# Reading back attention weights in whole rows, reordered first products and a shorter Newton chain in a hybrid decoder step

## The chip, the core and the metric

The kernel runs on one core of a Trainium2 chip. The core has TensorE (PE in the profile; its weight loads are PEld), VectorE (DVE), ScalarE (ACT), GpSimd (POOL) and SyncE (SP), which here issues nearly all transfers, and 16 DMA engines that move the data. The metric is the device time of one execution in microseconds; lower is better.

## What is computed

One layer of a decoder in float32, for a prompt of 512 tokens and for 8 running sequences ("samples") with one new token each. One projection of x (1024 columns) by `w_in` gives the inputs of two mixers; a second one by `w_out` and a layer norm end the layer:

```python
h = jnp.einsum('btd,de->bte', x, w_in)
qa, ka, va, za, ga, qb, kb, vb, gb = jnp.split(h, split_points, axis=-1)
log_a = log_sigmoid(za @ w_alpha2 + b_alpha) / GATE_TEMP
o_a, s_new = gla_chunked(qa, ka, va, log_a, s0, chunk)        # mixer A: gated linear attention, 4 heads
o_a = o_a * lax.rsqrt(jnp.mean(jnp.square(o_a), axis=-1, keepdims=True) + RMS_EPS) * gla_norm_g
o_b = dilated_attention(qb, k_all, v_all, q_idx, rel_bias)    # mixer B: 8 heads, three dilated windows
mix = jnp.concatenate([o_a * silu(ga), o_b * silu(gb)], axis=-1)
x_new = layer_norm(DEEPNORM_ALPHA * x + mix @ w_out, ln_g, ln_b)
```

In mixer B a sample's one query meets 256 cached keys per head (those that the three windows reach, gathered on the host in a fixed order) and its own new key. Its output is the sum of 256 cached value rows, weighted by the softmax.

## The kernel before

**Products in three parts.** Each float32 operand is split on the chip into a high part (`hi`, `xh`; ScalarE rounds to float32r) and a rest (`lo`, `xl`; VectorE subtracts), by `split` at line 412. A product is then three matmuls (`three`, line 608): high by high, high by rest, rest by high.

**The stages.** `dense` (line 681) is TensorE's main program: `ka` first, then the forget gate's `za`, then `qa`, `qb`, `kb`, `vb`, `gb`, `va`, `ga` and the output projection. For `ka` the loop goes over eight row blocks k of the contraction, and in each over two halves u of the tokens and two halves i of the columns, as their loads arrive (`first_loads` and `first_splits`, lines 536 and 563, with the list `FIRST`). All other weights come through two raw buffers (`weight_loads`, line 506): a load, the split, the next load. Beside this run the prompt's GLA (`gla_*`), its dilated attention (`strips`, `scores`, `softmax`, `weighted`, lines 1096 to 1208), and the samples' work.

**What sets the order.** Every piece of work is a generator that yields its instructions. `Plan.run` (line 300) keeps a model of the engines with a fixed cost for each instruction and each transfer (`Op`, line 77) and always issues the instruction that could begin first by that model, then the one of the lowest priority number. So the order on each engine is fixed when the program is built; on the chip an engine takes its instructions in that order, and one that waits holds those behind it. SyncE too has one order, and its transfers go into one queue on each DMA engine. All instructions are issued at line 359, so in the profile groups are told apart by the names of their tiles. Buffers come from pools of slots (`SLOTS`, line 58): a load waits until the slot's last user is done.

**The samples' attention.** `sample_queries` and `sample_logit` (lines 1211 and 1222) multiply cached keys with the queries on GpSimd and sum them on VectorE into `lt`. `sample_softmax` (line 1231) puts the logits together on TensorE (`ps_sl`), exponentiates and scales them: `p_s` has 64 partitions, row b*8 + h for sample b and head h, with 256 cached keys and one new one. Line 1269 stores it to the DRAM tile `psd_s`. `sample_values` (line 1284) then, for each sample `bi`, loads the cached values `vv` (128 partitions: h2*64 + d for head 2m + h2 and feature d; 4 x 256 elements for m and key) and the weights `pb` in the same layout, each row of weights repeated over 64 partitions: two loads, one for each h2. `sample_value` (line 1297) multiplies `vv` by `pb` on GpSimd in four pieces of 256, and VectorE sums over the keys into `o_pv`. `vv` and `pb` take two of the four `sv` slots, so two samples are in work at a time. After the eighth `o_pv`, `o_bs` and `mix_sample_b` follow; the output projection needs them, and also the samples' GLA (`sample_gla`, line 1307), whose buffers `s4` and `v4` use the same four slots.

A DRAM side of a transfer is written as a list of [step, count], outermost first. The attention bias strips, which `strips` loads to 128 partitions, have the side `[[T_P - 16, 8], [T_P - 1, 16], [1, w]]` (line 1107): 8 by 16 rows of w elements. The old `pb` loads have `[[0, 64], [512, 4], [1, 256]]`.

**The norms.** `rsqrt` (line 388) computes a reciprocal root as exp(-0.5 ln x) on ScalarE with one Newton step. For the layer norm of the prompt (`norm`, line 1560) the step is on ScalarE, while VectorE centres the rows (`between`); elsewhere it is on VectorE.

Of the kernel before, what the change touches and what calls it, by code (L numbers as in the profile page):

```python
# [11 lines left out]
F32 = mybir.dt.float32  # L12
# [10 lines left out]
KT = DM // P  # L23
# [29 lines left out]
T_D = 512  # L53
T_W = T_D + 258

N_WARM = 8

SLOTS = dict(
# [305 lines left out]
def trunk(ctx: ExitStack, tc: tile.TileContext, xT, xp, xs, state, ck, cv, w_in, wab, gnorm,  # L364
# [23 lines left out]
    def rsqrt(o, x, scale, eps, between=None):  # L388

        t = yield Need("m", "newton", [P, size(x)])  # L390
        t = t[:x.ap[0][1]]
        yield V.tensor_scalar(x, x, scale, eps, op0=ALU.mult, op1=ALU.add)
        yield S.activation(o, x, AF.Ln)
        yield S.activation(o, o, AF.Exp, scale=-0.5)
        if between:

            add(between, 5)
            yield S.activation(t, o, AF.Square)
            yield S.mul(t, t, x)
            yield S.activation(t, t, AF.Copy, scale=-0.5, bias=1.5)  # L400
            yield S.mul(o, o, t)
        else:
            yield V.tensor_tensor(t, o, o, op=ALU.mult)
            yield V.tensor_tensor(t, t, x, op=ALU.mult)
            yield V.tensor_scalar(x, o, -0.5, None, op0=ALU.mult)
            yield V.scalar_tensor_tensor(o, t, -3.0, x, op0=ALU.add, op1=ALU.mult)
        free(t)
# [31 lines left out]
    tabr = dram.tile([HB, T_R, T_P], F32, name="tabr")  # L439
    vad = dram.tile([NB, 512], F32, name="vad")  # L440
    qsd = dram.tile([NB, 512], F32, name="qsd")
    psd_s = dram.tile([64, 256], F32, name="psd_s")
    B = {}

    def make(key, need, n=1):
# [58 lines left out]
    order = [g for k, g in groups.items() if k not in ("ka0", "ka1")] + wo  # L504

    def weight_loads():
        for g in order:
            for i in range(g.parts):
                yield from g.load(i)

# [25 lines left out]
    def first_loads():  # L536
        za = w_in[:, OFF["za"]:OFF["za"] + 16].rearrange("(k p) n -> p k n", p=P)
        for n, a, *b in FIRST:
            if n == "x":
                c = b[0] if b else slice(0, NT)  # L540
                if a % 2 == 0 and c.start == 0:
                    xraw.append((yield Need("g", f"x_raw{a}", [P, 2, NT])))
                yield D.dma_start(xraw[a // 2][:, a % 2, c], xT[a * P:(a + 1) * P, c])
            else:
                if a % 4 == 0:
                    ka_raw.append((yield Need("r", f"raw_ka{a}", [P, 4, GW])))
                rows = w_in[a * P:b[0] * P, OFF["ka"]:OFF["ka"] + GW]
                yield D.dma_start(ka_raw[a // 4][:, a % 4:a % 4 + b[0] - a, :], rows.rearrange("(k p) n -> p k n", p=P))
            mark("first")
        yield D.dma_start(zw[:, :, :16], za)  # L550
        mark("zw")
        yield D.dma_start(cf, c_f[:, :C_E2])
        add(weight_loads(), 3)
        B["rb_raw"] = yield Need("t1", "rb_raw", [64, NB, HB])
        for i in range(2):
            yield D.dma_start(B["rb_raw"][i * 32:i * 32 + 32], rel_bias[:, None, :].to_broadcast([32, NB, HB]))
        yield D.dma_start(cm_w, c_m)
        mark("const")
        yield D.dma_start(gn, gnorm)
# [3 lines left out]
    def first_splits():  # L563
        for j, (n, a, *b) in enumerate(FIRST):
            yield At("first", j + 1)
            if n == "x":
                c = b[0] if b else slice(0, NT)
                if a % 2 == 0 and c.start == 0:
                    for l in (xh, xl):
                        y = yield Need("g", f"xx{a}", [P, 2, NT], F32R)  # L570
                        xt.append(y)
                        l += [y[:, 0, :], y[:, 1, :]]
                yield from split(xraw[a // 2][:, a % 2, c], xh[a][:, c], xl[a][:, c])
                mark("xs")
            else:
                if a % 4 == 0:
                    hl = []
                    for x in ("hi", "lo"):
                        hl.append((yield Need("w", f"{x}_ka{a}", [P, 4, GW], F32R)))
                    ka_hl.append(hl)  # L580
                    for i in range(2):
                        g = groups[f"ka{i}"]
                        for l, y in zip((g.hi, g.lo), hl):
                            l += [y[:, k, i * P:i * P + P] for k in range(4)]
                r = slice(a % 4, a % 4 + b[0] - a)
                yield from split(ka_raw[a // 4][:, r, :], *(y[:, r, :] for y in ka_hl[a // 4]))
                for _ in range(a, b[0]):
                    mark("kas")
                if b[0] % 4 == 0:
                    free(ka_raw[a // 4])  # L590
        add(weight_splits(), 4)
# [89 lines left out]
    def dense():  # L681
        for _ in range(N_WARM):
            yield T.matmul(warm_ps, warm[:, :P], warm, start=True, stop=True)
        free(warm_ps)
        free(warm)

        pk = {}
        for i in range(2):
            for u in range(2):
                pk[i, u] = yield bank("ds"[i], f"ps_ka{i}{u}")  # L690
        for k in range(KT):
            for u in range(2):
                yield At("kas", k + 1)
                yield At("xs", k + 1 + (u if k == 0 else 1))
                for i in range(2):
                    yield from three(pk[i, u][:, :TW[u]], k, halves(k, u, groups[f"ka{i}"]))
        for x in ka_hl:
            free(*x)

        pz = yield bank(("t", "s"), "ps_za")  # L700
        yield At("zw")
        yield Batch(T.matmul(pz[j * 32:j * 32 + 32, :QN[j]], zw[:, k, :], xraw[k // 2][:, k % 2, Q0[j]:Q0[j] + QN[j]],
                             start=k == 0, stop=k == KT - 1, skip_group_check=True)
                    for k in range(KT) for j in range(TT))
        free(zw, *xraw)
        add(gate_decay(pz), 10)
        yield from make("ka", Need("g", "ka", [P, 2, NP]), 3)
        yield from make("qa", Need("g", "qa", [P, 2, NP]), 2)
        for i in range(2):
            for u in range(2):  # L710
                add(into("ka", ka_s, i, 1.0)(pk[i, u], u), 2)
        for i in range(2):
            yield from feature(groups[f"qa{i}"], into("qa", qa_s, i, 0.125))
        for x in ("qh0", "ql0", "qh1", "ql1"):
            yield from make(x, Need("g", x, [P, 4, 256], F32R), 4)
        for i in range(4):
            yield from feature(groups[f"qb{i}"], parts("q", q_s, i, 0.125))
        for i in range(4):
            yield from make(f"kp{i}", Need("g", f"kp{i}", [P, 2, 512], F32R), 2)
            yield from feature(groups[f"kb{i}"], parts("k", k_s, i, 1.0))  # L720
        for i in range(2):
            for u in range(2):
                yield from make(f"vhl{i}{u}", Need("g", f"vhl{i}{u}", [P, 2, 4, 2, 64], F32R))
            yield from token(groups[f"vb{i}"], *vb_into(i))
        yield from gates("gb", gb_s)
        for u in range(2):
            yield from make(f"va{u}", Need("g", f"va{u}", [P, 2, 512]))
        for i in range(2):
            yield from token(groups[f"va{i}"], *va_into(i))
        yield from gates("ga", ga_s)  # L730
        free(*xt)
        for t in range(TT):
            add(residual(t), 8)
        add(residual_sample(), 8)
        units = [(g, f) for g in range(4) for f in range(2)]
        yield from out_first(*units[:5])
        for x in units[5:]:
            yield from out_first(x)
        for t, c, w in ((2, 0, 512), (2, 512, 512), (3, 0, 512), (3, 512, GW), (3, 768, GW)):
            yield from out_unit(t, c, w)  # L740
# [42 lines left out]
    def bias_table():  # L783
# [7 lines left out]
        tsb = yield Need("g", "tsb", [HB, T_P])  # L791
        yield V.memset(tsb[:, T_D:], NEG)
        yield At("rb")
        pt = yield bank("t", "ps_tab")
        yield T.matmul(pt[:HB, :T_D], rb[:, 0, :], ct, start=True, stop=True)
        yield copy(tsb[:, :T_D], pt[:HB, :T_D])
# [434 lines left out]
    def sample_softmax():  # L1231
# [34 lines left out]
        free(ps)  # L1266
        yield V.reciprocal(sum_s, sum_s)
        yield V.tensor_scalar(p_s, p_s, sum_s, None, op0=ALU.mult)
        yield D.dma_start(psd_s, p_s[:, :256])
        mark("psd_s")  # L1270
        yield V.tensor_scalar(pn_r, pnm, p_s[:, 256:257], None, op0=ALU.mult)
        free(p_s)
# [11 lines left out]
    def sample_values():  # L1284
        yield At("psd_s")
        for bi in range(NB):
            vv = yield Need("sv", f"vv{bi}", [P, 2, 512])
            yield D.dma_start(vv, cv[bi])
            pb = yield Need("sv", f"pb{bi}", [P, 4, 256])
            row = psd_s[bi * 8:bi * 8 + 8, :]  # L1290
            for h2 in range(2):
                yield D.dma_start(pb[h2 * 64:h2 * 64 + 64],
                                  bass.AP(tensor=row.tensor, offset=row.offset + h2 * 256, ap=[[0, 64], [512, 4], [1, 256]]))
            add(sample_value(bi, vv, pb), 20)
        mark("sv_free")

# [418 lines left out]
```

## Time and profile before

| what | before |
|---|---|
| median of 3 runs (lowest, highest) | 289.32 us (288.43, 290.51) |
| the profiled execution | 288.67 us |
| its span, first to last instruction | 286.8 us |
| mean granted TensorE clock | 0.994 |
| busy: PE, DVE, ACT, POOL | 275.0, 225.7, 167.5, 55.9 us |
| moved by DMA, mean rate | 51.18 MB, 178 GB/s |

A page of the profile gives each engine's busy time and its groups of instructions (out<-in by tile names, partitions x elements), with the idle time before them and what ended it. The chain of waits follows the work that ended last back to its start. The windows give, for a stretch of time, each engine's busy time, the clock, the mean busy share of the 16 DMA engines and the rate in GB/s; a share is counted by the packets that began in the stretch, so it can pass 1 a little. Times in the timelines are from the start of the span.

### The profile page before, as it was taken

The page shows a single profiled execution, that of the slowest core. Times are in us where ns is not written, and L with a number is a line of the kernel's source. Part 1 is how long each engine was busy: PE and PEld are TensorE (multiplying, and loading weights), DVE is VectorE, ACT ScalarE, POOL GpSimd, SP SyncE. Part 2 cuts the span into 40 slices and gives each one's busy share as a digit, 9 for nine tenths or more (in the row PEclk, how much of TensorE's full clock was granted, in tenths as well). Part 3 has the DMA queues.
Part 4 walks back from the last instruction along what each step waited for, and adds up shares of the span by engine and source line. Part 5 has one row for each costly group of instructions (what it writes and reads, how often), then busy time and mean ns, then how long its engine had stood idle before and what let it go on. Part 6 is the DMA issues. An engine that isn't in the chain of part 4 may idle for free.

```text
span 286.8 us, 6896 instructions
## 1 busy us (share of the span) xinstructions
PE 275.0 (96%) x2636; PEld 259.5 (90%) x2636; DVE 225.7 (79%) x547; ACT 167.5 (58%) x478; POOL 55.9 (19%) x74
## 2 busy tenths in 40 slices
PE   8999999999999998999999999999999999999990
PEld 5899999998989998899989999999999999997880
DVE  3846897999889968988889997864888995339745
ACT  5757664554567777566869867526689774113201
POOL 4000001000782444401604444540000000000000
PEclk9999999999999999999999999999999999999997
DMA  7966522225866797648998987559754788741211
GB/s 209 269 191 195 147 75 75 75 78 167 296 201 222 196 287 230 175 130 243 274 201 188 239 227 219 149 149 228 221 95 148 230 297 252 111 151 73 78 75 73
DMA packets 58936, 51.18 MB, mean 178 GB/s; under 512 B 12555, under 2 KB 50197, under 8 KB 58903
## 3 DMA queue, kind: packets, MB, share of 16 engines
q1 hardware_dynamic: 58794, 50.66, 63.2%
q8 instruction: 21, 0.34, 0.5%
q14 instruction: 13, 0.10, 0.1%
q10 hardware_dynamic: 108, 0.07, 0.1%
HBM read 45.17 MB, written 6.03 MB: 179 GB/s over the span
## 4 chain that ended last, share of the span: by engine, by line
PE 71%; DVE 13%; DMA 8%; ACT 5%; issue 2%; SPq 1%; DVEq 0%; ACTq 0%
PE ps_qb L359 8%; PE ps_yf L359 8%; PE ps_y L359 8%; PE ps_ga L359 6%; PE ps_kb L359 4%; PE ps_qa L359 4%; PE ps_gb L359 4%; PE ps_va L359 4%; PE ps_ka L359 4%; DMA raw_gb__2152<-in_w_in_dram 3%; DMA out_dram<-feat 3%; PE ps_pt L359 2%; PE ps_va_f L359 2%; PE ps_l L359 2%; PE ps_s L359 2%; PE ps_pv L359 2%
## 5 line engine op out<-in xcount | busy, mean ns | idle before, releaser
L359 POOL TENSOR_TENSOR vv<-vv,pb 128x256 f32<-128x256 f32 x32 | 26.1, 846 | 45.5 <-DMA pb<-psd_s 39.8
L359 POOL TENSOR_TENSOR past<-past,qbc 128x256 f32<-128x256 f32 x32 | 25.6, 831 | 43.4 <-DMA past<-in_ck_dram 36.0
L359 ACT ACTIVATE pr<-pr,ms 128x128 f32<-128x128 f32 (+3 forms) x49 | 26.1, 546 | 5.8 <-DVE ms L359 5.2
L359 PE MATMUL ps_pt<-cf,pr 128*128 128x128 f32 x80 | 14.1, 280 | 1.4 <-DVE pt L359 1.0
L359 DVE CUSTOM_DVE_ANT_0 pr<-ps_s,strip 128x128 f32<-128x128 f32 (+3 forms) x32 | 14.3, 476 | 0.0
L359 PE MATMUL ps_ka<-xx,hi_ka 128*128 128x264 f32 (+1 forms) x64 | 13.5, 307 | 0.3 <-DVE xx L359 0.3
L359 ACT ACTIVATE sg<-sg 128x264 f32<-128x264 f32 (+1 forms) x32 | 13.4, 419 | 0.2
L359 PEld LDWEIGHTS ps_ka<-xx,hi_ka 128*128 128x128 f32 x64 | 11.0, 205 | 1.2 <-DVE xx L359 0.8
L359 DVE TENSOR_TENSOR ptl<-ps_pt,pth 128x384 fp32r<-128x384 f32 (+1 forms) x16 | 9.8, 617 | 2.8 <-ACT pth L359 2.8
L359 PEld LDWEIGHTS ps_pt<-cf,pr 128*128 128x128 f32 x80 | 9.0, 140 | 3.3 <-DVE pt L359 1.6
L359 ACT ACTIVATE d<-d 128x512 f32<-128x512 f32 x13 | 7.8, 637 | 6.7 <-DVE d L359 6.7
L359 ACT COPY feat_y<-ps_yf 128x256 f32<-128x256 f32 x8 | 3.0, 371 | 12.7 <-PE ps_yf L359 12.7
L359 ACT ACTIVATE rstd<-mv 128x1 f32<-128x1 f32 x4 | 0.7, 199 | 15.9 <-DVE mv L359 15.9
L359 POOL MEMSET att<- 64x512 f32 x2 | 1.0, 523 | 44.5 <-DVE ks L359 44.5
L359 ACT CAST pth<-ps_pt 128x384 fp32r<-128x384 f32 (+1 forms) x16 | 8.4, 534 | 2.2 <-PE ps_pt L359 2.0
L359 DVE TENSOR_REDUCE o_pv<-vv 128x4 f32<-128x1024 f32 x8 | 9.7, 1212 | 0.0
L359 DVE TENSOR_REDUCE lt<-past 128x16 f32<-128x1024 f32 x8 | 9.6, 1199 | 0.0
L359 PE MATMUL ps_ka<-xx,lo_ka 128*128 128x264 f32 (+1 forms) x32 | 9.4, 295 | 0.0
L359 DVE TENSOR_TENSOR obT<-ps_pv,pvl 64x256 f32<-64x256 f32 x16 | 6.6, 415 | 3.5 <-ACT pvl L359 3.3
L359 DVE TENSOR_TENSOR xx<-x_raw,xx 128x520 fp32r<-128x520 f32 (+2 forms) x9 | 5.8, 640 | 4.6 <-ACT xx L359 4.6
L359 ACT COPY pvl<-ps_pv 64x256 f32<-64x256 f32 x16 | 5.5, 370 | 6.1 <-PE ps_pv L359 5.3
L359 DVE TENSOR_TENSOR d<-b 128x1024 f32<-128x1024 f32 x7 | 8.5, 1218 | 0.0
(535 smaller groups left out, 1092.4 us busy)
## 6 DMA issues: line engine op xcount, KB each, us to landing
past<-in_ck_dram SPq DMA_DIRECT2D x8, 512.0 KB
vv<-in_cv_dram SPq DMA_DIRECT2D x8, 512.0 KB
pb<-psd_s SPq DMA_DIRECT2D x16, 256.0 KB
qbc<-qsd SPq DMA_DIRECT2D x8, 256.0 KB
strip<-tabr SPq DMA_DIRECT2D x8, 256.0 KB
y<-in_xp_dram SPq DMA_DIRECT2D x4, 512.0 KB
x_raw<-in_xT_dram SPq DMA_DIRECT2D x7, 260.0 KB
out_dram<-y SPq DMA_DIRECT2D x3, 512.0 KB
```

What stands on the lines that cost most here:

```text
L359: getattr(eng.eng, op.fn)(*op.args, **op.kw)
```

## The change

Four edits, and an order that the planner makes anew from them:

- `psd_s` becomes [8, 2, 1024]: for each sample and h2 one row with the weights of the four heads 2m + h2. `p_s` is stored to it in two transfers (even and odd partitions). A `pb` load is one transfer instead of two, with the DRAM side [[1024, 2], [0, 64], [1, 1024]]: two rows of 4 KB, each repeated over 64 partitions.
- In the `ka` products of a row block, the two high-part matmuls with `xh` (by `hi` and by `lo`) of both column halves come first, those with `xl` last; the second and third row block of x are split in token halves too (`N_HALF`).
- The first half of the queries' weights (`qa`) is loaded ahead of `zw`, `cf` and the other constants; the bias table's product waits until the first `qa` half is evacuated.
- In `rsqrt` with `between`, x is scaled by -0.5 beforehand, and the Newton step's product with x and its affine step become one ScalarE instruction that takes x as its scale.

```diff
+N_HALF = 3
 def rsqrt(o, x, scale, eps, between=None):
         t = t[:x.ap[0][1]]
-        yield V.tensor_scalar(x, x, scale, eps, op0=ALU.mult, op1=ALU.add)
-        yield S.activation(o, x, AF.Ln)
-        yield S.activation(o, o, AF.Exp, scale=-0.5)
         if between:
+            yield V.tensor_scalar(x, x, eps, -0.5, op0=ALU.add, op1=ALU.mult)
+            yield S.activation(o, x, AF.Ln, scale=-2.0)
+            yield S.activation(o, o, AF.Exp, scale=-0.5)
             add(between, 5)
             yield S.activation(t, o, AF.Square)
-            yield S.mul(t, t, x)
-            yield S.activation(t, t, AF.Copy, scale=-0.5, bias=1.5)
+            yield S.activation(t, t, AF.Copy, scale=x, bias=1.5)
             yield S.mul(o, o, t)
         else:
+            yield V.tensor_scalar(x, x, scale, eps, op0=ALU.mult, op1=ALU.add)
+            yield S.activation(o, x, AF.Ln)
+            yield S.activation(o, o, AF.Exp, scale=-0.5)
...
-    psd_s = dram.tile([64, 256], F32, name="psd_s")
+    psd_s = dram.tile([NB, 2, 1024], F32, name="psd_s")
...
     def weight_loads():
-        for g in order:
+        for g in order[1:]:
...
             mark("first")
+        yield from order[0].load(0)
         yield D.dma_start(zw[:, :, :16], za)
...
-                yield from split(xraw[a // 2][:, a % 2, c], xh[a][:, c], xl[a][:, c])
-                mark("xs")
+                for c in (c,) if b or a >= N_HALF else TS:
+                    yield from split(xraw[a // 2][:, a % 2, c], xh[a][:, c], xl[a][:, c])
+                    mark("xs")
...
                 yield At("kas", k + 1)
-                yield At("xs", k + 1 + (u if k == 0 else 1))
-                for i in range(2):
-                    yield from three(pk[i, u][:, :TW[u]], k, halves(k, u, groups[f"ka{i}"]))
+                yield At("xs", 2 * k + 1 + u if k < N_HALF else k + 1 + N_HALF)
+                for last in (False, True):
+                    for i in range(2):
+                        pairs = halves(k, u, groups[f"ka{i}"])
+                        for j in (1,) if last else (0, 2):
+                            yield T.matmul(pk[i, u][:, :TW[u]], *pairs[j], start=k == 0 and j == 0, stop=k == KT - 1 and last)
...
         yield At("rb")
+        yield At("qa_done", 1)
         pt = yield bank("t", "ps_tab")
...
-        yield D.dma_start(psd_s, p_s[:, :256])
+        for h2 in range(2):
+            src = bass.AP(tensor=p_s.tensor, offset=p_s.offset + h2 * p_s.ap[0][0], ap=[[2 * p_s.ap[0][0], 32], [1, 256]])
+            yield D.dma_start(psd_s[:, h2].rearrange("b (m k) -> b m k", m=4), src)
         mark("psd_s")
...
             pb = yield Need("sv", f"pb{bi}", [P, 4, 256])
-            row = psd_s[bi * 8:bi * 8 + 8, :]
-            for h2 in range(2):
-                yield D.dma_start(pb[h2 * 64:h2 * 64 + 64],
-                                  bass.AP(tensor=row.tensor, offset=row.offset + h2 * 256, ap=[[0, 64], [512, 4], [1, 256]]))
+            row = psd_s[bi]
+            yield D.dma_start(pb, bass.AP(tensor=row.tensor, offset=row.offset, ap=[[1024, 2], [0, 64], [1, 1024]]))
             add(sample_value(bi, vv, pb), 20)
```

The edits shift the planner's order on every engine. Three places matter for what follows. First, SyncE's queue around the store of the weights; before:

```order
L359 DMA psd_s<-p_s 64x256
L359 DMA vv_2070<-in_cv_dram 128x1024
L359 DMA out_dram<-vb_raw 128x256
L359 DMA pb_2082<-psd_s 64x4x256 x2
L359 DMA vv_2119<-in_cv_dram 128x1024
L359 DMA pb_2129<-psd_s 64x4x256 x2
L359 DMA raw_gb__2152<-in_w_in_dram 128x8x128
```

and after:

```order
L360 DMA raw_gb__2122<-in_w_in_dram 128x8x128
L360 DMA out_dram<-vb_raw 128x256
L360 DMA raw_va__2146<-in_w_in_dram 128x4x256
L360 DMA psd_s<-p_s 8x4x256 x2
L360 DMA strip_2241<-tabr 128x1x512
L360 DMA strip_2268<-tabr 128x1x512
L360 DMA vv_2255<-in_cv_dram 128x1024
L360 DMA pb_2295<-psd_s 128x1x1024
L360 DMA vv_2304<-in_cv_dram 128x1024
L360 DMA pb_2317<-psd_s 128x1x1024
L360 DMA raw_va__2312<-in_w_in_dram 128x4x256
```

The store now stands behind the last `gb` and the first `va` weights, and two strips stand between it and the first `vv`. (Between the later `pb` loads come one more strip, two more halves of `va` and one `ga`.)

Second, VectorE around `p_s`; before:

```order
L359 TENSOR_SCALAR pr_1920<-pr_1920,ms_1943 128x512
L359 TENSOR_REDUCE mx_s<-ps_sl 64x1
L359 RECIPROCAL sum_s<-sum_s 64x1
L359 TENSOR_SCALAR p_s<-p_s,sum_s 64x257
L359 TENSOR_TENSOR obT_2015<-ps_pv_2016,pvl_2038 64x256
```

and after:

```order
L360 TENSOR_TENSOR gb_2099<-ps_gb_0_2101,sg 128x256
L360 TENSOR_TENSOR gb_s<-ps_gb_0_2101,sg 128x8
L360 TENSOR_TENSOR gb_2099<-gb_2099,obT_1711 128x256
L360 TENSOR_TENSOR ptl_2066<-ps_pt_2161,pth_2060 128x4x128
L360 TENSOR_REDUCE mx_s<-ps_sl 64x1
L360 TENSOR_TENSOR mlb_2180<-gb_2099,mhb_2179 128x256
L360 ISA pr_2184,ms_2220<-ps_s_2188,strip_1636 128x384
L360 ISA ms_2220 128x1
L360 RECIPROCAL sum_s<-sum_s 64x1
L360 ISA pr_2186,ms_2222<-ps_s_2190,strip_1946 128x384
L360 ISA ms_2222 128x1
L360 TENSOR_SCALAR p_s<-p_s,sum_s 64x257
```

`p_s` now stands behind the first `gb` evacuation and two 384-wide score rows (ISA, in the profile CUSTOM_DVE_ANT_0), which stood behind it before. On TensorE, `ps_sl` stands behind 95 more products than before: 37 of `ps_gb`, 28 of `ps_vb`, 16 of `ps_pv` and 14 transposes.

Third, VectorE at the last sums of the samples' values; before:

```order
L359 TENSOR_REDUCE o_pv<-vv_2706 128x4
L359 TENSOR_TENSOR obT_2855<-ps_pv_2901,pvl_2922 64x256
L359 TENSOR_TENSOR gb_2135<-gb_2135,obT_2855 128x256
L359 TENSOR_TENSOR mlb_2419<-gb_2135,mhb_2340 128x256
L359 TENSOR_TENSOR lo_va__2963<-raw_va__2683,hi_va__2962 128x512 x2
L359 TENSOR_TENSOR lo_ga__2975<-raw_ga__2785,hi_ga__2974 128x1024
L359 TENSOR_REDUCE o_pv<-vv_2819 128x4
L359 MEMSET qx 128x512
L359 TENSOR_TENSOR qx<-qa_s,cf 128x4x2x2 x2
L359 TENSOR_REDUCE o_pv<-vv_2915 128x4
L359 TENSOR_TENSOR vnt<-vnt,o_pv 128x32
L359 TENSOR_TENSOR lo_ga__3120<-raw_ga__2977,hi_ga__3119 128x1024
```

and after:

```order
L360 TENSOR_REDUCE o_pv<-vv_2781 128x4
L360 TENSOR_TENSOR lo_va__2959<-raw_va__2645,hi_va__2958 128x512 x2
L360 TENSOR_TENSOR lo_ga__2971<-raw_ga__2832,hi_ga__2970 128x1024
L360 TENSOR_REDUCE o_pv<-vv_2884 128x4
L360 MEMSET qx 128x512
L360 TENSOR_TENSOR qx<-qa_s,cf 128x4x2x2 x2
L360 TENSOR_REDUCE o_pv<-vv_2937 128x4
L360 TENSOR_TENSOR vnt<-vnt,o_pv 128x32
L360 TENSOR_TENSOR gb_s<-gb_s,vnt 128x32
L360 TENSOR_TENSOR mlb_2180<-gb_s,mhb_2179 128x4x8
L360 TENSOR_TENSOR lo_ga__3120<-raw_ga__2973,hi_ga__3119 128x1024
L360 TENSOR_TENSOR lo_ga__3124<-raw_ga__2989,hi_ga__3123 128x1024
```

The sixth `o_pv` moved by three rows; the seventh and eighth stand where they stood, and behind the eighth come, as before, the splits of the second and third `ga` weights and the GLA state.

## The prediction

> **What bounds the kernel now.** The page first: which engine fills the span, and what the chain that ended last is made of.
>
> ```profile
> span 286.8 us, 6896 instructions
> PE 275.0 (96%) x2636; PEld 259.5 (90%) x2636; DVE 225.7 (79%) x547; ACT 167.5 (58%) x478; POOL 55.9 (19%) x74
> PE 71%; DVE 13%; DMA 8%; ACT 5%; issue 2%; SPq 1%; DVEq 0%; ACTq 0%
> L359 POOL TENSOR_TENSOR vv<-vv,pb 128x256 f32<-128x256 f32 x32 | 26.1, 846 | 45.5 <-DMA pb<-psd_s 39.8
> ```
>
> TensorE is busy nearly throughout, so an edit elsewhere gains only where TensorE waits for it, and loses wherever it makes TensorE wait. The last row is the place to watch: GpSimd idles 39.8 us waiting for `pb` loads, at no cost so far. Those loads are what the change rewrites. When the work on them ran shows in the timelines of GpSimd and VectorE (start, duration):
>
> ```profile
> 134.84 2.86 POOL L359 TENSOR_TENSOR vv<-vv,pb 128x256 f32<-128x256 f32 x4 [16.69 <-DMA pb<-psd_s]
> 186.04 3.68 POOL L359 TENSOR_TENSOR vv<-vv,pb 128x256 f32<-128x256 f32 x4 [0.78 <-DMA pb<-psd_s]
> 126.03 0.35 DVE L359 TENSOR_SCALAR p_s<-p_s,sum_s 64x257 f32<-64x257 f32 x1
> 189.75 1.22 DVE L359 TENSOR_REDUCE o_pv<-vv 128x4 f32<-128x1024 f32 x1
> ```
>
> From `p_s` at 126 to the eighth `o_pv`, which ends at 190.97, eight batches pass. VectorE takes its instructions in program order, so a late `o_pv` holds everything behind it: the splits of the last gate weights, the GLA state and output work, the evacuations.
>
> How many DMA engines a load uses is read from stretches in which one kind of load moves. SyncE's timeline tells which kind:
>
> ```profile
> 120.32 1.72 SPq L359 DMA_DIRECT2D strip<-tabr  x2
> 123.03 0.66 SPq L359 DMA_DIRECT2D out_dram<-vnt_rows  x1
> 129.56 1.32 SPq L359 DMA_DIRECT2D pb<-psd_s  x2
> 130.97 0.55 SPq L359 DMA_DIRECT2D vv<-in_cv_dram  x1
> 227.95 0.89 SPq L359 DMA_DIRECT2D y<-in_xp_dram  x2
> 235.09 0.46 SPq L359 DMA_DIRECT2D gamma<-in_ln_g_dram  x1
> 235.65 0.38 SPq L359 DMA_DIRECT2D beta<-in_ln_b_dram  x1
> 27.08 0.38 SPq L359 DMA_DIRECT2D raw_qb__434<-in_w_in_dram  x1
> ```
>
> Between 120.32 and 123.03 only two strip loads are issued. The windows, each some us after such issues (PE, PEld, DVE, ACT, POOL busy; clock; share of the 16 DMA engines; GB/s), are for the strips, the old `pb` halves, `gamma` and `beta`, `y`, and 512-byte weight rows:
>
> ```profile
> 122.00:123.20 1.20, 1.20 (x12) 1.20 (x11) 1.17 (x3) 1.20 (x6) 0.00 (x0) 1.00 0.50 183
> 131.80:133.20 1.40, 1.40 (x15) 1.24 (x13) 1.40 (x4) 1.17 (x2) 0.00 (x0) 1.00 1.05 209
> 240.30:241.20 0.90, 0.90 (x10) 0.90 (x9) 0.00 (x0) 0.22 (x1) 0.00 (x0) 1.00 1.06 405
> 231.00:233.00 2.00, 2.00 (x19) 2.00 (x19) 2.00 (x6) 2.00 (x7) 0.00 (x0) 1.00 1.05 429
> 29.30:30.00 0.70, 0.70 (x8) 0.70 (x8) 0.61 (x2) 0.64 (x3) 0.00 (x0) 1.00 1.14 345
> ```
>
> The strips, though two are in flight, hold exactly half of the engines; the others hold all. What differs is the access: a strip's DRAM side is [8][16][w], outermost count 8; those of the old `pb` halves begin with 64, of `gamma`, `beta`, `y` and the weights with 128. Eight outermost rows, eight engines; and two such loads share the same eight, or the share would be 1. One engine moves 183/8 = 22.9 GB/s in 1 or 2 KB rows, 405/(16x1.06) = 23.9 to 429/(16x1.05) = 25.5 in 4 KB rows, 345/(16x1.14) = 18.9 in 512 B rows.
>
> **The change part by part.** *The `pb` load.* Before, two loads whose DRAM side began with [0, 64]; after, one whose DRAM side is [2][64][1024]: outermost count 2. Read as the strips were, it runs on two engines, always the same two. That is 262,144 bytes an engine, 262.1/25.5 = 10.3 us, where all sixteen would take 1.3 us. The price is bounded below by the nearest row, eight engines (2.6 us), above by two at 23.9 GB/s (11.0 us). I take 10.3: the row shows engines equal to the outermost count, and 2 is that count here.
>
> The Trainium skill, "DMA: Bandwidth & Descriptors", section "Why a DMA increments its semaphore by 16 and not by 1", states that the number of engines is the largest up to 16 that divides the slowest dimension of both sides, the lowest-numbered ones. By that rule the load has two engines, and the sum is the one below; the trace agrees for 8, and no row shows 2.
>
> SyncE's queue is one, and every load with 128 outermost rows has its sixteenth on each of those two engines, so it lands only after the `pb` loads ahead of it. I follow what these two engines must move, from the order after the change: the two stores of `psd_s`, two strips, then vv, pb eight times, with a strip, three halves of `va` and one `ga` between.
>
> *Where it starts.* TensorE's `ps_sl`, from which `p_s` comes, stood at 123.64 in the chain of waits; now 95 more products of TensorE stand ahead of it (37 of `ps_gb`, 28 of `ps_vb`, 16 of `ps_pv`, 14 transposes).
>
> ```profile
> 123.64 0.90 PE ps_sl L359 x7
> 128.58 0.44 PE ps_pt L359 x4
> 154.06 0.97 PE ps_gb L359 x8
> 134.93 0.55 DVE L359 CUSTOM_DVE_ANT_0 pr<-ps_s,strip 128x384 f32<-128x384 f32 x1
> 136.02 0.55 DVE L359 CUSTOM_DVE_ANT_0 pr<-ps_s,strip 128x384 f32<-128x384 f32 x1
> ```
>
> At 0.11 to 0.12 us each that is 11 us: 134.6. On VectorE `p_s` now follows the two 384-wide score rows that ran at 134.93 and 136.02, plus about 1.5 us of `gb` rows: 138. So `psd_s` is issued at about 138.3 (126.4 before), with 4 us of doubt. A load's first bytes come some 3 us after its issue:
>
> ```profile
> 2.60 3.77 DMA x_raw<-in_xT_dram
> ```
>
> (260 KB, 0.65 us of its own.) The two engines so begin on the strips at about 142. Then 8 x (10.3 + 32.8/25.5 = 1.3 for `vv`) = 92.7; three strips 3 x 1.4 = 4.3; three `va` halves at 1.6, between the 2 KB and 512 B rates, 4.8; one `ga` 1.7: 103.5 us, to 245.5. No gap opens in between: slots for the batch after next come free 4.3 us after a landing (3.1 of products, 1.2 of reduction), while the next `pb` still has 6 us to go. After the last landing 3.1 and 1.2 follow: the eighth `o_pv` ends at 249.8, against 190.97: **58.8 us late**.
>
> *What of it is given back.* While VectorE waits, TensorE can run ahead as far as banks and split weights reach. From there on the program order is the old one:
>
> ```profile
> 190.00:230.00 40.00, 39.70 (x378) 38.32 (x378) 29.75 (x105) 30.07 (x110) 0.00 (x0) 1.00 0.64 174
> ```
>
> VectorE and ScalarE need 30 of these 40 us, so at most 10 can be caught up; waits among them remain, and I take **7**, with 0 and 10 as ends.
>
> *First products.* TensorE waited for the rests of x at the second and third row block:
>
> ```profile
> 7.80 0.39 PE L359 MATMUL ps_ka<-xx,hi_ka 128*128 128x264 f32 x1 [0.34 <-DVE xx L359]
> 9.52 0.19 PEld L359 LDWEIGHTS ps_ka<-xx,hi_ka 128*128 128x128 f32 x1 [0.21 <-DVE xx L359]
> ```
>
> Rests last, and halves split apart, take these away: **-0.6 us** (at most 0.7 in the quoted waits and a slow product beside them; a loss of 0.3 if the two more splits on ScalarE delay the next weights).
>
> *Queries' weights first; table product later.* The weights come before `zw`, `cf` and the small constants: four of the latter are issued later by one weight load (0.4 us of SyncE, 1.7 of the engines). They are wanted at 18.23:
>
> ```profile
> 18.23 2.05 PE L359 MATMUL ps_za<-x_raw,zw 128*32 128x128 f32 x64
> 18.27 1.15 DVE L359 TENSOR_TENSOR lo_qa__265<-raw_qa__174,hi_qa__264 128x1024 fp32r<-128x1024 f32 x1
> 20.21 0.40 PE L359 MATMUL ps_tab<-ct,rb 66*8 66x512 f32 x1
> ```
>
> The split of the weights already ended at 19.42 under `ps_za`; earlier brings nothing, and `zw`, issued at 8.56, keeps several us in hand. The table product moves behind thirty `ps_qa` products; its strips are loaded from 68 on. Zero, hidden by `ps_za` and by 30 us; if `zw` came late, at most 1 us.
>
> *Newton chain.* At the end the last tile waits for it:
>
> ```profile
> 281.41 0.29 ACT L359 ACTIVATE newton<-newton,mv 128x1 f32<-128x1 f32 x1
> 281.74 0.20 ACT L359 ACTIVATE newton<-newton 128x1 f32<-128x1 f32 x1
> 281.97 0.29 ACT L359 ACTIVATE rstd<-rstd,newton 128x1 f32<-128x1 f32 x1
> 282.30 1.41 DVE L359 SCALAR_TENSOR_TENSOR y<-y,rstd,beta 128x512 f32<-128x512 f32 x2 [0.31 <-ACT rstd L359]
> ```
>
> Two instructions, a product with `mv` and an affine step, become one with a tensor scale: 0.23 us less, inside VectorE's 0.31 us wait: **-0.2**. One issue of 0.6 us less per batch on SyncE is hidden: the data, not the issue, is late.
>
> *Sum.* 286.8 + 58.8 - 7 - 0.6 - 0.2 = 337.8 us of span. The profiled execution took 288.67 us, 1.9 more than its span, so **340 us** with rounding; the median of the runs, 289.32, is 0.65 above that execution.
>
> **Rivals.** *All engines, or eight, after all (not slower).* If the queue spreads the load over eight engines or more, the load takes 1.3 to 2.6 us; a batch then needs 2.6 + 1.3 + 3 of latency + 4.3 = 11.2 us, two run at once, so 8 x 5.6 = 45 us from 142 end at 187, before the old 190.97. Nothing waits; the small gains stand: 286.8 - 0.8 + 1.9 = 288 us, inside 1%, the bound of what a measurement of this kernel can tell from no change. For it: the old halves ran on all (1.05), and a load's bytes are the same. Against: the strips' share of 0.50.
>
> The Trainium skill's table "Rules for kernel authors" on the same page supports this side: two transfers to disjoint partition halves serialize on the same engines and should be one transfer. By it the change costs nothing, 288 us; the same table warns of a small outermost count, which the strips' 0.50 bears out.
>
> *Two engines, chosen anew for each load.* Two batches then move side by side: 10.3 + 1.3 + 3 + 4.3 = 18.9 us for two, four times from 142: 218, 27 late; less 7 given back and 0.8, 306 us. Against: two strips in flight held the same eight.
>
> *The queue itself stalls.* If a load's many packets for one engine block the issue of what follows, `vv` and weights start only after it, 3 us of latency eight times: 364 us. The trace has no row for it.
>
> **How the numbers follow.** Forecast 0.82; all or eight engines 0.07; chosen anew 0.06; stalled issue 0.05. The forecast's own range: start 4 us either way, give-back 0 to 10, rate up to 5.6 us more: 328 to 354. 326 to 354 leaves out the three rivals, 0.18. Slower by over 1%: 0.82 + 0.06 + 0.05 = 0.93. The 0.07 of the first rival lies at 288, 0.3% under the time before: 0.05 within 1%, 0.02 faster for gains that I have put too low.
>
> **What would show it.** Right: stretches between 150 and 240 with a DMA share near 2/16 and some 50 GB/s; GpSimd's wait for `pb` near 60 us or more; an `o_pv` every 11 to 13 us, the last ending near 250; TensorE idle some tens of us; `ps_yf` starting near 280; the tail after it as before. Wrong: a share near 1 while `pb` moves, or `pb` landing within 5 us. If the last `o_pv` is at 250 but the end is not at 338, the give-back was wrong; if it is elsewhere, the start or the rate.

## The result, and the profile after

The changed kernel takes 350.75 us (median of 6 runs, 349.49 to 351.94), the kernel before 289.44 us beside it (6 runs, 287.96 to 290.51): 1.213 times as long, with a 95% interval of 1.208 to 1.217. 340 us was forecast, with a range of 326 to 354. Ratios and their intervals leave out single executions that ran over 1.5% above the fastest of the same kernel; medians do not. The profiled execution of the changed kernel took 349.49 us, and its page begins:

```profile
span 347.6 us, 6876 instructions
PE 286.7 (82%) x2636; PEld 270.3 (78%) x2636; DVE 219.5 (63%) x546; ACT 169.4 (49%) x479; POOL 51.3 (15%) x74
PE 51%; DMA 30%; DVE 7%; ACT 4%; POOL 3%; issue 2%; SPq 1%; POOLq 0%; DVEq 0%; ACTq 0%
L360 DVE TENSOR_REDUCE o_pv<-vv 128x4 f32<-128x1024 f32 x8 | 9.8, 1221 | 66.0 <-POOL vv L360 66.0
L360 POOL TENSOR_TENSOR vv<-vv,pb 128x256 f32<-128x256 f32 x32 | 22.3, 727 | 109.8 <-DMA pb<-psd_s 109.8
```

TensorE fell from 96% of the span to 82%, and transfers from 8% of the chain of waits to 30%. GpSimd's wait for `pb` grew from 39.8 to 109.8 us, and now it costs: VectorE's eight reductions stand 66.0 us behind it, where the same group of before has 0.0. From 142 to 250 TensorE waits above all for results of VectorE (us in total, times, longest):

```profile
PE ps_pv L360 <- DVE ptl L360: 14.8, 2, 8.9
PE ps_va_f L360 <- DVE lo_va__2959 L360: 9.8, 1, 9.8
PE ps_pt L360 <- DVE ptl L360: 7.2, 1, 7.2
```

SyncE's timeline and, below it, GpSimd's eight batches (start, duration):

```profile
138.45 1.26 SPq L360 DMA_DIRECT2D psd_s<-p_s  x2
142.97 0.97 SPq L360 DMA_DIRECT2D pb<-psd_s  x1
143.99 10.73 SPq L360 DMA_DIRECT2D raw_va__2312<-in_w_in_dram  x1
154.76 5.27 SPq L360 DMA_DIRECT2D strip<-tabr  x1
```

```profile
157.89 2.77 POOL L360 TENSOR_TENSOR vv<-vv,pb 128x256 f32<-128x256 f32 x4 [35.66 <-DMA pb<-psd_s]
170.13 2.77 POOL L360 TENSOR_TENSOR vv<-vv,pb 128x256 f32<-128x256 f32 x4 [9.47 <-DMA pb<-psd_s]
185.69 2.79 POOL L360 TENSOR_TENSOR vv<-vv,pb 128x256 f32<-128x256 f32 x4 [12.80 <-DMA pb<-psd_s]
199.37 2.76 POOL L360 TENSOR_TENSOR vv<-vv,pb 128x256 f32<-128x256 f32 x4 [10.88 <-DMA pb<-psd_s]
213.63 2.81 POOL L360 TENSOR_TENSOR vv<-vv,pb 128x256 f32<-128x256 f32 x4 [11.50 <-DMA pb<-psd_s]
225.53 2.77 POOL L360 TENSOR_TENSOR vv<-vv,pb 128x256 f32<-128x256 f32 x4 [9.08 <-DMA pb<-psd_s]
239.77 2.82 POOL L360 TENSOR_TENSOR vv<-vv,pb 128x256 f32<-128x256 f32 x4 [11.48 <-DMA pb<-psd_s]
251.50 2.76 POOL L360 TENSOR_TENSOR vv<-vv,pb 128x256 f32<-128x256 f32 x4 [8.90 <-DMA pb<-psd_s]
```

A batch comes every 11.7 to 15.6 us. The windows (busy PE, PEld, DVE, ACT, POOL; clock; DMA share; GB/s) tell what moves between two bursts of other loads:

```profile
148.00:154.00 6.00, 6.00 (x54) 6.00 (x54) 4.84 (x19) 5.60 (x16) 0.00 (x0) 1.00 0.13 53
234.00:237.00 3.00, 3.00 (x28) 2.99 (x26) 0.00 (x0) 0.82 (x3) 0.00 (x0) 1.00 0.13 52
142.00:250.00 108.00, 67.18 (x498) 64.03 (x496) 40.14 (x94) 34.73 (x92) 19.49 (x28) 0.84 0.35 113
```

0.13 is 2/16: two engines, each at some 26 GB/s (53/2), while fourteen rest. In the 108 us from 142 to 250 TensorE was busy for 67.18.

That a wide load's part waits on these two engines shows in the sizes of their packets. The `va` weights issued at 143.99, in rows of 1 KB, move on the free engines by 158. From 166.0 to 168.4 the two engines still move rows of 4 KB alone, the rest of the second `pb`; from 168.4 to 169.9 rows of 1 KB follow, again at a share of 0.13 (the packets under 512 B carry 4 bytes and no rows):

```profile
DMA packets 31, 0.13 MB, mean 53 GB/s; under 512 B 0, under 2 KB 0, under 8 KB 31
DMA packets 47, 0.07 MB, mean 47 GB/s; under 512 B 2, under 2 KB 39, under 8 KB 47
```

### The profile page after: what moved, and what is told of

It is laid out like the page before. It is cut to its first block, busy times and chain, and to the rows that moved or that the text cites. A ratio compares the mean times of both kernels' runs of the same rounds, so it can differ in the third digit from the quotient of the medians.

```text
span 347.6 us, 6876 instructions
## 1 busy us (share of the span) xinstructions
PE 286.7 (82%) x2636; PEld 270.3 (78%) x2636; DVE 219.5 (63%) x546; ACT 169.4 (49%) x479; POOL 51.3 (15%) x74
## 4 chain that ended last, share of the span: by engine, by line
PE 51%; DMA 30%; DVE 7%; ACT 4%; POOL 3%; issue 2%; SPq 1%; POOLq 0%; DVEq 0%; ACTq 0%
DMA pb<-psd_s 27%; PE ps_kb L360 7%; PE ps_yf L360 7%; PE ps_qb L360 7%; PE ps_y L360 7%; PE ps_qa L360 3%; POOL vv L360 3%; PE ps_ka L360 3%; PE ps_vb L360 2%; PE ps_l L360 2%; PE ps_vb_f L360 2%; PE ps_oa L360 2%; DMA x_raw<-in_xT_dram 2%; PE ps_s L360 1%; PE ps_ga L360 1%
## 5 line engine op out<-in xcount | busy, mean ns | idle before, releaser
L360 POOL TENSOR_TENSOR vv<-vv,pb 128x256 f32<-128x256 f32 x32 | 22.3, 727 | 109.8 <-DMA pb<-psd_s 109.8
L360 PE MATMUL ps_pt<-cf,pr 128*128 128x128 f32 x80 | 15.4, 301 | 12.5 <-DVE ptl L360 7.2
L360 PE MATMUL ps_pv<-ptl,vhl 128*64 128x256 f32 (+1 forms) x32 | 8.4, 304 | 14.8 <-DVE ptl L360 14.8
L360 PEld LDWEIGHTS ps_pt<-cf,pr 128*128 128x128 f32 x80 | 10.1, 152 | 12.0 <-issue 11.1
L360 PEld LDWEIGHTS ps_pv<-ptl,vhl 128*64 128x64 f32 x32 | 5.0, 155 | 15.2 <-DVE ptl L360 15.2
L360 ACT CAST mhb<-gb 128x256 fp32r<-128x256 f32 x8 | 3.2, 401 | 20.4 <-DVE gb L360 20.4
L360 PE MATMUL ps_kv<-va,kt 128*64 128x128 f32 x32 | 2.4, 298 | 12.6 <-ACT va L360 12.6
L360 PEld LDWEIGHTS ps_kv<-va,kt 128*64 128x64 f32 x32 | 1.8, 145 | 13.0 <-ACT va L360 12.8
L360 PE MATMUL ps_va_f<-xx,lo_va__2959 128*128 128x264 f32 x8 | 3.0, 373 | 9.8 <-DVE lo_va__2959 L360 9.8
L360 PEld LDWEIGHTS ps_va_f<-xx,lo_va__2959 128*128 128x128 f32 x8 | 2.0, 254 | 10.0 <-DVE lo_va__2959 L360 10.0
```

Source lines behind the costliest of these rows:

```text
L360: getattr(eng.eng, op.fn)(*op.args, **op.kw)
```

## Experiments

In the first four the order is that of the changed kernel, instruction by instruction: the planner still prices one load, and in its place two loads of 64 partitions go out, whose DRAM side is varied.

**Two loads, outermost count 64** (of the edit, the list that changes).

```diff
-ap=[[1024, 2], [0, 64], [1, 1024]]            # one load
+ap=[[0, 64], [1, 1024]]                       # two loads, offsets 0 and 1024
```

> The changed kernel; each pb is read with the same whole 4 KB rows from the same place of memory, but as two loads of 64 partitions each, DRAM side [0, 64][1, 1024] (outermost count 64 in place of 2). Every other instruction is where the changed kernel has it. Theory A (the outermost count of the DRAM side sets the number of DMA engines): all sixteen take part, a batch's pb moves in about 1.3 us, the eighth o_pv ends between 187 and 195 and the time is 288.5 us (287 to 291). Rival B (what is slow is that 64 partitions read one and the same 4 KB row, whatever the count): the eighth o_pv stays near 255 and the time near 350. Rival C (the later p_s and the other edits carry a part of the loss): 295 to 320.

Measured: 295.03 us, ratio 1.016 (1.011 to 1.020). The last `o_pv` starts at 200.5, against 254.29 in the changed kernel, and GpSimd idles 2 to 6 us before a batch instead of 9 to 13. From 142 to 203 all DMA engines are busy:

```profile
142.00:203.00 61.00, 55.92 (x468) 54.11 (x467) 44.58 (x97) 35.47 (x94) 24.81 (x32) 1.00 1.00 218
```

The loss falls from 61 to about 5 us (4.5 by the ratio, 5.3 by the spans of the profiled executions, 292.1 and 286.8). So the DRAM side makes up some 56 us of the change, and something else, which was not in the forecast, about 5. Theory A is right about the engines and missed the time: the eighth `o_pv` ends at 201.7, not by 195, and 295 lies at the lower end of Rival C. Where the 5 us lie shows beside the kernel before (first the two windows of before, then those of this run):

```profile
80.00:90.00 10.00, 9.78 (x85) 9.29 (x85) 9.15 (x28) 6.21 (x22) 6.57 (x9) 1.00 0.60 181
150.00:180.00 30.00, 29.78 (x247) 28.32 (x246) 28.17 (x69) 23.17 (x63) 12.78 (x16) 1.00 0.86 219
```

```profile
80.00:90.00 10.00, 10.00 (x99) 9.52 (x98) 6.69 (x21) 5.99 (x18) 2.68 (x4) 0.86 0.07 13
150.00:180.00 30.00, 24.92 (x207) 23.77 (x207) 25.92 (x61) 20.19 (x55) 12.99 (x16) 1.00 1.02 208
```

```profile
79.05 0.27 PE L361 MATMUL ps_pt<-cf,pr 128*128 128x128 f32 x1 [1.91 <-issue]
```

Between 80 and 90 TensorE's clock is at 0.86, after the wait of 1.91 us that the third fence shows. This need not come with the order: the run with count 8 below has the same order, and its clock is 1.00 there. Between 150 and 180 TensorE idles 5 us, all of it for `ptl` of VectorE:

```profile
PE ps_pv L361 <- DVE ptl L361: 3.9, 2, 2.2
PE ps_pt L361 <- DVE ptl L361: 1.2, 1, 1.2
```

The kernel before has no listed wait on TensorE in that stretch. The work is the same; the order is not.

**Outermost counts 2, 4 and 8.** Same two loads, same bytes, same rows:

```diff
-ap=[[0, 64], [1, 1024]]
+ap=[[0, k], [0, 64 // k], [1, 1024]]          # k = 2, 4, 8
```

> As the run with two loads of outermost count 64, but the DRAM side of each of the two loads is written [0, 2][0, 32][1, 1024]: outermost count 2, same rows, same bytes, same number of loads. Theory A: two engines again, DMA share 0.13 while only pb moves, about 350 us (346 to 354). Rival B': it is the single load of 128 partitions that is slow, two of 64 are not: 288.5 us.

> The same with [0, 4][0, 16][1, 1024]: outermost count 4. Theory A: four engines, share 0.25 while only pb moves, 5.1 us for a batch's pb; the four engines have 8 x 5.1 + 26 for the other loads (the 26 that the changed kernel's trace gives: 108 us from 142 to 250, less 8 x 10.3) = 67 us, from 142 to 209, the eighth o_pv ends about 213, 22 later than before; less 4 to 7 given back: 305 us (299 to 311). Rival (any split count behaves like the fast or the slow case): 288.5 or 350.

> The same with [0, 8][0, 8][1, 1024]: outermost count 8. Theory A: eight engines, share 0.5 while only pb moves, 2.6 us for a batch's pb; two buffers and 4.3 us of products and reduction then set the pace, 8 x 5.6 = 45 us from 142, the eighth o_pv ends at 187 to 197 and the time is 289 us (287 to 294). Rival (loss proportional to 1/count with no cover: 62 us x (1/8) / (1/2)): 304 us.

| outermost count | us | ratio (95%) | last `o_pv` starts | DMA share and GB/s between bursts of other loads |
|---|---|---|---|---|
| 2 | 351.88 | 1.217 (1.212 to 1.221) | 256.5 | 0.13, 52 |
| 4 | 313.51 | 1.082 (1.078 to 1.086) | 217.3 | 0.26, 97 |
| 8 | 297.09 | 1.027 (1.023 to 1.031) | 202.6 | 0.50, 150 |
| 64 | 295.03 | 1.016 (1.011 to 1.020) | 200.5 | 1.03, 198 (with `vv`) |

A window of each, for the counts 2, 4, 8 and 64:

```profile
183.00:187.00 4.00, 4.00 (x36) 3.70 (x33) 2.53 (x11) 3.64 (x11) 0.00 (x0) 1.00 0.13 52
```

```profile
171.00:173.00 2.00, 2.00 (x18) 1.50 (x17) 2.00 (x5) 0.48 (x1) 0.00 (x0) 1.00 0.26 97
```

```profile
177.00:179.00 2.00, 0.60 (x5) 0.39 (x4) 0.93 (x1) 0.11 (x1) 1.04 (x2) 1.00 0.50 150
```

```profile
145.00:153.00 8.00, 8.00 (x69) 7.43 (x68) 7.28 (x25) 6.90 (x20) 1.57 (x2) 1.00 1.03 198
```

For 2, 4 and 8, as many engines as the outermost count. Two loads of count 2 cost what one of count 2 costs (351.88, 350.75), so it is not the single load that is slow; nor is it the 4 KB row, which the run with 64 reads too. From 2 to 4 the last `o_pv` moves by 39.2 us; eight loads at half the duration should give 8 x 5.15 = 41. From 4 to 8 it moves by 14.7, less than the 20.6 that the engines save, and from 8 to 64 by 2.1. One reason stands in the windows: an engine moves 52/2 = 26 GB/s, then 97/4 = 24, 150/8 = 19 and 198/(16 x 1.03) = 12, so the more engines read the repeated rows, the less each of them moves. On sixteen engines `gamma` and `beta` moved 405 GB/s. Whether the repetition is the cause was not tested, and the pace of buffers and products may have its part too. The times for 4 and 8 are 8 us above what was expected. Some 5 of them belong to this order, as the expectation took the kernel before as its base; the rest was not taken apart.

By the rule of the Trainium skill, "DMA: Bandwidth & Descriptors", section "Why a DMA increments its semaphore by 16 and not by 1" (the largest number up to 16 that divides the slowest dimension of both sides), it would be 2, 4, 8 and 16 engines; the shares agree for 2, 4 and 8. The other side's rule, in the table "Rules for kernel authors" on the same page of the Trainium skill, that two transfers to disjoint partition halves should become one, costs some 56 us here, as the one transfer has the smaller outermost count.

**The parts alone.** Four kernels start from the kernel before, so the planner makes an order for each.

*All edits but that on `psd_s` and `pb`:*

> The kernel before with every edit but the one on psd_s and pb (first products, queries' weights first, table product later, Newton chain). Theory A' (the 5 us that the run with two loads of outermost count 64 still loses come from the order: these edits put ps_sl 84 instructions of TensorE later, and the products wait in other places): 293.5 us (291 to 297), ps_yf starting near 235 instead of 230. Rival, the forecast's own terms (these edits are worth -0.8 together and the 5 us belong to the reading of whole 4 KB rows): 288.5 us (287.5 to 289.5).

Measured: 299.39 us, ratio 1.035 (1.030 to 1.039). The small edits cost 10 us, more than either side expected, and elsewhere: `ps_yf` starts at 229.2, before the expected 235, but then TensorE waits. Its longest wait there is for `o_r` of the samples' GLA, whose buffers use the slots of the samples' values; the last `o_pv` comes at 218.85 (189.75 before). That the one comes from the other is read from the slots, not tested:

```profile
230.00:250.00 20.00, 14.63 (x115) 12.87 (x114) 13.59 (x35) 11.51 (x31) 0.00 (x0) 0.87 0.98 275
244.22 0.30 PE L360 MATMUL ps_ort<-cf,o_r 128*128 128x128 f32 x1 [2.25 <-DVE o_r L360]
```

*The `psd_s` and `pb` edit alone:*

> The kernel before with the edit on psd_s and pb alone (one load of outermost count 2), in which ps_sl and p_s stay where the kernel before has them (p_s at 126 instead of 138). Theory A: psd_s is issued at 126.4, 12 us earlier than in the changed kernel; the two engines have the same 108 us of work, so the eighth o_pv ends about 243.5 (52.5 later than before); 3.6 to 7 given back: 337 us (332 to 342). Rival (something other than the two engines' queue sets the pace, so that an early start brings nothing): 350 us.

Measured: 349.27 us, ratio 1.208 (1.202 to 1.214); the expectation missed. `psd_s` is issued at 126.49, the eighth `o_pv` ends at 247.84, so the way from the one to the other takes 121.4 us instead of 117.1: a `gb` half, another `va` half and two stores of `vb_raw` now stand in it too. The rival's number, 350, came out, though not its reason: the early start does bring the eighth `o_pv` 7.7 us forward, and 5.6 of these are lost again before `ps_yf`, as the windows further below show. By this run the `psd_s` and `pb` edit alone costs 60 us and by the one above all the others alone 10, together 61: the parts do not add up.

*Rests last alone, and whole rows as two loads with the Newton chain* (planned as two loads):

> The kernel before with the edit on the first products alone (rests of x last, their splits two at a time for the first three row blocks). The forecast's term: -0.6 us, 288.8 us. Rival, read from the changed kernel's trace (TensorE idles 0.20 and 0.91 us for ScalarE's cast of x where it idled 0.34 before): +0.8 us, 290.2 us. Either way inside 1%; TensorE's idle time in the first 12 us tells them apart.

> The kernel before with p_s stored by pairs and read back in whole 4 KB rows, but as two loads of 64 partitions (outermost count 64), and with the shorter Newton chain; no other edit, and ps_sl where the kernel before has it. Theory A: all sixteen engines, a batch's pb in 1.3 us as before, nothing waits, -0.2 from the Newton chain: 289 us (288 to 290.5), same as before. Rival (whole 4 KB rows read by 64 partitions cost time of their own): 292 us or more.

Measured: 289.02 us, ratio 0.9985 (0.9962 to 1.0008), and 288.91 us, ratio 0.9996 (0.9966 to 1.0026). Neither can be told from no change. Both keep `ps_sl` where the kernel before has it: it is the 1373rd product of TensorE in all three traces (row 1097 as the expectations count). The idle time of TensorE does not settle the first term: in the first 12 us it waits 0.24 and 1.17 us for x with rests last, 0.52, 0.35 and 0.35 in the run without that edit, 0.34 in the profile of before. Among the runs with rests last it differs as much, from no such wait (all edits but that on `psd_s` and `pb`) to 1.62 us (g3 below).

**Which edit moves the order.**

```diff
 # g1: changed kernel, pb as two loads of count 64, and
-        yield from order[0].load(0)      # queries' weights ahead of constants
 # g2: kernel before, and
+        yield from order[0].load(0)
 # g3: g1, and
-        yield At("qa_done", 1)           # table product later
```

(and `order` in place of `order[1:]`, or the reverse, in `weight_loads`).

> The changed kernel with pb as two loads of outermost count 64, and with the edit on the queries' weights undone (they are loaded after the small constants again); rests last, table product later and the Newton chain stay. ps_sl then stands at row 1087 of TensorE instead of 1183, where the kernel before has 1097. Theory O (the 5.7 us that the two-loads run still lost come from the order, and of the small edits it is the queries' weights that moved it): 289 us (287.5 to 291). Rival (the rests, the table product or the reading of whole rows carry them): 293 us or more.

> The kernel before with one edit: the first half of the queries' weights is loaded ahead of the small constants. ps_sl stands at row 1194 of TensorE instead of 1097. Theory O: 295 us (292 to 301), TensorE idle or at a lower granted clock between 70 and 90 and again after 150. Rival, the forecast's term (zero, hidden): 289.3 us.

> The changed kernel with pb as two loads of outermost count 64 and without the edits on the queries' weights and the table product: rests last, whole rows and the shorter Newton chain are left, ps_sl at row 1097 as in the kernel before. Theory O: 288.7 us (287.5 to 290). Rival (the planner's lower price for the one load alone costs time by the order it leads to): 291 us or more.

Measured: g1 296.27 us, ratio 1.023 (1.018 to 1.029); g2 301.92 us, ratio 1.043 (1.038 to 1.048); g3 293.46 us, ratio 1.014 (1.009 to 1.019). g2 bears Theory O out in kind: the queries' weights alone do cost 12 us by the order, more than its 295. Of the places that the theory names, the first counts for little: from 70 to 90 the clock is 1.00 and TensorE is busy for 18.38 us, against 19.50 before. More is lost late, after `ps_yf` has begun at 232.0: from 240 to 252, where the kernel before has no idle time, TensorE is busy for 7.50 of 12 us:

```profile
240.00:252.00 12.00, 7.50 (x58) 5.91 (x59) 6.93 (x21) 6.08 (x20) 0.00 (x0) 0.79 0.72 214
```

For g1 and g3 the theory's times missed and the rivals' ranges hold: without the queries' weights 6 to 7 us are still lost, and without the table product as well, 4. g3 and the run of whole rows as two loads (f4) differ only in rests last (nothing by itself) and in the planner's price for `pb`, one load or two; what goes out for `pb` is the same. TensorE's stretch from 140 to 170, f4 first and then g3:

```profile
140.00:170.00 30.00, 29.89 (x253) 28.52 (x252) 28.07 (x65) 24.31 (x61) 9.40 (x12) 1.00 1.01 217
```

```profile
140.00:170.00 30.00, 26.11 (x214) 23.98 (x214) 26.48 (x61) 20.46 (x51) 13.87 (x16) 1.00 0.96 241
```

So a price in the planner, alone or together with rests last, moves 3.8 us of idle time into TensorE, with no change in what goes out for `pb`. No version beat the kernel before. Which single rows of the orders cost what stays open.

## Why the prediction was right, and where it was not

**Two engines, and which transfers queue behind them: right.** The share is 0.13, and 0.13, 0.26 and 0.50 for counts of 2, 4 and 8; `psd_s` is issued at 138.45, forecast 138.3, and `ps_sl` and `p_s` stand where the working has them. The Newton chain saves what was worked out: three ScalarE steps at the end are now two between `Square` and `y`, and from the step that takes `mv` to the start of `y` 0.65 us pass (342.53 to 343.18) instead of 0.89 (281.41 to 282.30). In the time of the kernel this is too little to be seen.

```profile
342.29 0.20 ACT L360 ACTIVATE newton<-rstd 128x1 f32<-128x1 f32 x1
342.53 0.29 ACT L360 ACTIVATE newton<-newton,mv 128x1 f32<-128x1 f32 x1
342.86 0.29 ACT L360 ACTIVATE rstd<-rstd,newton 128x1 f32<-128x1 f32 x1
343.18 1.41 DVE L360 SCALAR_TENSOR_TENSOR y<-y,rstd,beta 128x512 f32<-128x512 f32 x2
```

**The length of the queue: 6 us too short.** GpSimd starts its last batch at 251.50, where the forecast had the last landing at 245.5. Of this, 1.5 us stand at the first batch: 142, two strips and 11.6 us for `vv` and `pb` give 156.4, and GpSimd starts at 157.89, as the forecast has no time between a load's last byte and the engine that waits for it. The seven steps from batch to batch take 93.6 us, where the forecast's terms give 89.1. Where only `vv` and `pb` stand between two batches, a step is 11.7 to 12.2 us against 11.6, so `pb` itself was priced well. Where a `va`, a `ga` or a strip stands there too, it is 13.7 to 15.6 against 13.2 to 14.6, so those loads cost 0.5 to 1.1 us more than counted each time; why was not tested. The eighth `o_pv` ends at 255.51 rather than 249.8.

**What is given back: the step that failed.** 7 us were to be caught up. From the last `o_pv` to `ps_yf` the changed kernel takes 3.6 us less than before, half of the forecast, and even these are not caught up by the stall, as a comparison within the same order shows. The windows from the end of the eighth `o_pv` to the first `ps_yf`, of before, of the changed kernel, of the run with two loads of count 64, and of the `pb` edit alone:

```profile
190.97:229.80 38.83, 38.53 (x368) 37.15 (x368) 28.62 (x103) 29.43 (x108) 0.00 (x0) 1.00 0.64 173
```

```profile
255.50:290.70 35.20, 31.99 (x276) 30.51 (x277) 28.79 (x104) 28.09 (x104) 0.00 (x0) 0.88 0.63 176
```

```profile
201.70:235.30 33.60, 32.76 (x319) 31.39 (x318) 28.55 (x104) 28.09 (x104) 0.00 (x0) 1.00 0.65 178
```

```profile
247.84:288.70 40.86, 40.03 (x364) 38.89 (x365) 29.30 (x104) 29.47 (x107) 0.00 (x0) 0.94 0.60 163
```

Even without a stall this order needs only 33.6 us there, as it has 319 products left instead of 368. The stall lets TensorE run ahead by 43 more (276 left); at 32.76/319 = 0.103 us each that is 4.4 us. Yet the stretch is 1.6 us longer. TensorE idles 2.4 us more (35.20 - 31.99 against 33.60 - 32.76), and at the clock of 0.88 its 276 products take 31.99 us, 3.6 more than at 0.103 each. These are estimates, as the products left are not all of one size. So TensorE did run ahead, and idle time and clock took more than that away. In the run of the `pb` edit alone hardly a product ran ahead (364 left, 368 in the kernel before), and the stretch is 2 us longer than before; its order was made anew too, so this is a near comparison and not one of the same order. The forecast's two errors in size (queue too short, give-back too large) point the same way, hence 340 and not 351.

**A new order costs nothing: failed.** The forecast priced the moved `p_s` and the cover of each edit, but not that the planner's order as a whole changes. "Zero, hidden by `ps_za` and by 30 us" was wrong: the queries' weights alone cost 12 us, and with two loads of count 64 the order of the changed kernel costs about 5. Behind the two engines most of this may be hidden: the run of the `pb` edit alone, in another order, is only 1.5 us faster than the changed kernel. Rests last, at -0.6, is neither shown nor refuted (between -1.1 and +0.2 us by its interval).

**The rivals.** All or eight engines: refuted by the share. With such a DRAM side 295 to 297 is what they give, not 288: the eighth `o_pv` ends at 201.7, not 187. This rival's price of 1.3 us for a `pb` on sixteen engines was too low by the forecast's own row for the old halves, 209 GB/s, which makes 2.5 us (524.3/209); with 64, 198 GB/s over `vv` and `pb` together make 2.6 or more, by estimate. Engines chosen anew: refuted, since from 148 to 154 the first two batches' loads, issued at 141.78 and 142.97, are both in flight, and the share is 0.13, not 0.25. (The 306 us of this rival are its span; 1.9 more make the time.) A stalled issue: SyncE does stall, 10.73 us on one weight load. But this is not the mechanism of 364 us: in no single microsecond from 142 to 250 is the DMA share below 0.11, so the two engines always have work, later issues start nothing later on them, and the latency does not add up. On the other fourteen the weights do start later; what this costs by itself was not separated.

**The sum.** In the forecast's own terms: 286.8 + 64.5 for the late `o_pv` (58.8 forecast) - 3.6 given back (7) - 0.1 behind `ps_yf` (the small gains were to be 0.8) = 347.6. Split by experiments: 286.8 + 5.3 for the order (span of the two-loads run, 292.1) + 55.5 for the two engines. The ends of the forecast's own range do not follow from its terms: 340 - 4 - 3 and 340 + 4 + 7 + 5.6 make 333 to 357.

## What to carry to other kernels

Before two transfers are merged, write down the outermost count of both sides: where it falls below 16, as with 2, 4 and 8 here, the transfer loses engines, and every wide load queued behind it lands only when its share on the same few engines has passed. The engines gained at the other end are not all worth the same: from 8 to 64 brought 2 us. A stall's price is to be taken against the same order of instructions, and an edit that makes a planner choose again must be priced as a new order, by holding the order fixed once and letting it move once. What a stalled engine can catch up is counted in instructions that do not depend on the late data, less what idle time and clock take away behind it.

## What was not expected of the hardware

TensorE's clock halves in a gap that the stall opens, and takes time to come back. TensorE's first products after the eighth `o_pv`, and the windows around them:

```profile
258.43 0.70 PE L360 MATMUL ps_kv<-va,kt 128*64 128x128 f32 x4 [12.61 <-ACT va L360]
```

```profile
256.00:260.00 4.00, 1.57 (x8) 1.24 (x9) 3.00 (x6) 4.00 (x10) 0.00 (x0) 0.50 0.62 147
260.00:264.00 4.00, 4.00 (x23) 3.78 (x23) 3.30 (x13) 1.00 (x4) 0.00 (x0) 0.52 0.92 277
264.00:270.00 6.00, 6.00 (x63) 5.64 (x59) 4.25 (x20) 4.47 (x24) 0.00 (x0) 1.00 1.02 247
```

After 12.61 us of idle the granted clock is 0.50, and it stays at 0.52 for the next 4 us of full work: 23 products in 4 us, against 63 in the 6 us after. The Trainium skill, "TensorE: Matmul & The Clock Gate", section "Part 1: The HAM clock gate (the "warmup" mystery)", has the half clock after an idle window and the full one after a busy window of about 3.4 us, where the windows run freely and do not begin with the work. Here some 5.5 us passed from 258.43 to the full clock, less than two such windows.

And SyncE's issue of a transfer is not always short: the weight load behind the second `pb` took 10.73 us to issue, though fourteen engines were free, and nine later issues up to 252 took 2.4 to 10.4 us each. In the kernel before no transfer that stands alone in SyncE's timeline from 20 to 236 took over 1 us to issue. What holds the issue is not shown.
